# Two softmax attentions in a Trainium2 kernel: the heads taken one at a time, or two at a time in the two halves of the TensorE array

## The chip, the cores and the metric

The kernel runs on one core of one Trainium2 chip. The metric is the device time of one execution in microseconds (us). Times are medians of several runs; the rows shown come from one more execution, taken by the hardware profiler.

## What is computed

The program computes two transformer blocks on 256 tokens of width 1024, in fp32. Only the attention of the second block matters here. Two groups of 8 heads of 64 channels each attend causally over the 256 tokens; the second group adds a decay made of the cumulated logarithms of a forget gate:

```python
    s_own = jnp.einsum('bhcd,bhld->bhcl', qi, k_own).astype(jnp.float32) * scale
    s_own = jnp.where(causal, s_own, -jnp.inf)
    p = jax.nn.softmax(jnp.concatenate([s_sel, s_own], axis=-1), axis=-1)
...
    c = jnp.cumsum(log_f, axis=-1)
...
        s = (jnp.einsum('bhqd,bhkd->bhqk', qi, k).astype(jnp.float32) * scale
             + cq[..., None] - c[:, :, None, :])
        s = jnp.where(kpos[None, :] <= qpos[:, None], s, -jnp.inf)
        p = jax.nn.softmax(s, axis=-1).astype(v.dtype)
        return jnp.einsum('bhqk,bhkd->bhqd', p, v)
```

With 256 tokens there is one block of keys, so the first group is plain causal attention.

## The kernel before, in words

**The dense layers.** `linear` multiplies activations with weights that stream from HBM in units of 128x1024 numbers. ScalarE rounds a unit into a high part (`whi`, L204), VectorE, or GpSimd where `pool_k` says so, subtracts it into a low part (`wlo`, L207, L209), and TensorE forms every product in three passes of 256 columns (L229 to L231, `mm`). A unit is 24 such matmuls. The buffers `raw`, `whi` and `wlo` hold three units each.

**The attention steps.** The attention is a generator. `spawn(generator, rate)` puts it beside the dense layers; after each unit `linear` calls `tick(1/2)`, which adds half of the rate to a counter and runs one step of the generator, up to its next `yield`, for each whole number in it. `drain` runs what is left. So a step's instructions stand between two units of the dense layer, and a scheduler then orders each engine's instructions. The first attention (heads A, tiles `qa`, `ka`, `vta`) runs beside the layer that makes `qb`, `kb` and the values `vtb`; the second (heads B, tiles `qb`, `kb`, `vtb`) beside the layer that makes the gates `gt`. Head h has its 64 channels in rows 0 to 63 of chunk h // 2 if h is even, in rows 64 to 127 if it is odd.

**One step before** works at four heads at once, as a pipeline:

- scores of head h (L1319): 128 queries against 128 keys and 128 queries against 256 keys, with 64 of the array's 128 rows. For B the gate follows into the same PSUM tile (L1321), with 40 rows. The products are of full fp32 numbers, and each stands in the trace as two instructions.
- transposes of head h - 2 (L1326), three of 128x128, copied from PSUM by ScalarE (L1328).
- softmax of head h - 1: VectorE scales and masks out of PSUM (L1333), takes row extremes (L1336), ScalarE exponentiates with sums (L1337), VectorE inverts the sums and scales (L1339, L1341).
- value products of head h - 3 (L1348, L1349): the 64 channels of an even head come out in columns 0 to 63 of the array, of an odd head in columns 64 to 127. After an odd head the pair's sums are split into `oh` and `ol` (L1351, L1352).

```python
            if h < 8:
                c, par = divmod(h, 2)
                R, F = slice(64 * par, 64 * par + 64), slice(64 * par, 64 * par + 40)
```

**The gate's preparation.** `fox_c` (L1285) turns the eight gate rows into cumulated sums on VectorE (L1296, L1297) and ends in two rounds of a VectorE scaling `fw` (L1302), a GpSimd product `selh` over 8x2048 numbers (L1303), and a VectorE scaling `frh` (L1304). On VectorE these stand between the weight units and the first softmaxes of A.

Of the kernel before, what the change touches and what calls it, by code (L numbers as in the profile page):

```python
# [8 lines left out]
FT = mybir.dt.float32  # L9
# [4 lines left out]
AF = mybir.ActivationFunctionType  # L14
OP = mybir.AluOpType
AX = mybir.AxisListType
PSUM = bass.MemoryType.PSUM

P = 128
S = 256  # L20
# [140 lines left out]
class Kernel:  # L161
# [511 lines left out]
    def wkv(self, psum, pw, pA, y):  # L673
# [103 lines left out]
        for n in range(2):  # L777
            yield
            for src, dst in ((bt, mb[n]), (kt, mk[n])):
                for par in range(2):  # L780
                    R = slice(64 * par, 64 * par + 64)
                    ps = psum.tile([P, 2, 2 * P], FT, name="ax")
                    for c in range(2):
                        T.matmul(ps[:, c, :], src[R, c, n * P:(n + 1) * P],
                                 ar[R, c, n].rearrange("p a b -> p (a b)"), start=True, stop=True)
                    V.copy_predicated(dst[:, par], mskb, ps)
# [52 lines left out]
        for n in range(2):  # L839
# [4 lines left out]
            for par in range(2):  # L844
                R = slice(64 * par, 64 * par + 64)
                yp = psum.tile([P, 2, 64], FT, name="ax")
                for c in range(2):
                    T.matmul(yp[:, c, :], mk[n][:, par, c, 0:P], vh(par, c), start=True, stop=n == 0)
                    if n:
                        T.matmul(yp[:, c, :], ar[R, c, n, 0, :], st[R, c, :], start=False, stop=True)  # L850
                SC.activation(ys[:, par], yp, AF.Copy)
# [7 lines left out]
            if n == 0:  # L859
                sp = psum.tile([P, 2, 64], FT, name="ax")  # L860
                for c in range(2):
                    for par in range(2):
                        R = slice(64 * par, 64 * par + 64)
                        T.matmul(sp[R, c, :], bk[:, 0, c, R], us[:, par, c, :], start=True, stop=False)
# [307 lines left out]
    def block2_mix(self):  # L1172
        nc, tc = self.nc, self.tc
        V, SC, G, T = nc.vector, nc.scalar, nc.gpsimd, nc.tensor
        psum = self.psum
        with tc.tile_pool(name="pd", bufs=1) as pd:
# [3 lines left out]
            rot, ct, st, amask = atc[:, 0:128], atc[:, 128:384], atc[:, 384:640], atc[:, 640:1024]  # L1180
# [7 lines left out]
            qa, ka, qb, kb = (t(n, [P, 4, S]) for n in ("qa", "ka", "qb", "kb"))  # L1188
            vt = {n: t("vt" + n, [P, 2, 512]) for n in "ab"}
            gt = t("gt", [P, 16, S])  # L1190
            oh, ol = t("oh", [P, 2, 4, S], FR), t("ol", [P, 2, 4, S], FR)
# [51 lines left out]
            self.selh = selh  # L1243
            self.linear(psum, hh, hl, 12, 8, evac, outer=True)
            self.linear(psum, hh, hl, 1, 8, lambda n, ps: evac(n + 12, ps), groups=[1])
            self.spawn(self.attention(psum, pd, qa, ka, vt["a"], amask, None, oh[:, 0], ol[:, 0]), 1.5)
            self.linear(psum, hh, hl, 12, 8, lambda n, ps: evac(n + 13, ps))
            self.drain()
            self.spawn(self.attention(psum, pd, qb, kb, vt["b"], amask, self.fox, oh[:, 1], ol[:, 1]), 1.2)
            self.linear(psum, hh, hl, 16, 8, lambda n, ps: evac(n + 25, ps))  # L1250
            merged = t("mg", [P, 8, S])
            mh, ml = t("mh", [P, 8, S], FR), t("ml", [P, 8, S], FR)
# [54 lines left out]
    def attention(self, psum, pd, q, k, vt, amask, fox, oh, ol):  # L1307
        nc = self.nc
        V, SC, G, T = nc.vector, nc.scalar, nc.gpsimd, nc.tensor
        parts = ((0, 128), (128, 256))  # L1310
        sp, s, pp, op = {}, {}, {}, {}
        for step in range(8 + 3):
            h = step
            if h < 8:
                c, par = divmod(h, 2)
                R, F = slice(64 * par, 64 * par + 64), slice(64 * par, 64 * par + 40)
                sp[h] = psum.tile([P, 384], FT, name="ax")
                for i, (o, n) in enumerate(parts):
                    T.matmul(sp[h][:, o:o + n], q[R, c, i * P:(i + 1) * P], k[R, c, 0:n], start=True, stop=fox is None)  # L1319
                    if fox:  # L1320
                        T.matmul(sp[h][:, o:o + n], fox[0][F, h, i * P:(i + 1) * P], fox[1][F, 0:n], start=False, stop=True)  # L1321
            h = step - 2
            if 0 <= h < 8:
                pp[h] = psum.tile([P, 384], FT, name="ax")
                for b in range(3):
                    T.transpose(pp[h][:, b * P:(b + 1) * P], s[h][:, b * P:(b + 1) * P], self.ident)  # L1326
                pt = pd.tile([P, 384], FT, name="pt", bufs=3)
                SC.activation(pt, pp[h], AF.Copy)  # L1328
                pp[h] = pt
            h = step - 1  # L1330
            if 0 <= h < 8:
                s[h] = pd.tile([P, 384], FT, name="sc", bufs=3)
                V.scalar_tensor_tensor(s[h], sp[h], -0.125, amask, op0=OP.mult, op1=OP.add)  # L1333
                mx = pd.tile([P, 4], FT, name="mx", bufs=3)
                for i, (o, n) in enumerate(parts):
                    V.tensor_reduce(mx[:, i:i + 1], s[h][:, o:o + n], axis=AX.X, op=OP.min)  # L1336
                    SC.activation(s[h][:, o:o + n], s[h][:, o:o + n], AF.Exp, bias=mx[:, i:i + 1], scale=-1.0,  # L1337
                                  accum_out=mx[:, 2 + i:3 + i])
                V.reciprocal(mx[:, 2:4], mx[:, 2:4])  # L1339
                for i, (o, n) in enumerate(parts):  # L1340
                    V.tensor_scalar(s[h][:, o:o + n], s[h][:, o:o + n], mx[:, 2 + i:3 + i], None, op0=OP.mult)  # L1341
            h = step - 3
            if 0 <= h < 8:
                c, par = divmod(h, 2)
                R = slice(64 * par, 64 * par + 64)
                if par == 0:
                    op[c] = psum.tile([P, S], FT, name="ax")
                T.matmul(op[c][R, :], vt[:, 0, h * 64:(h + 1) * 64], pp[h][:, 0:256], start=True, stop=False)  # L1348
                T.matmul(op[c][R, 128:256], vt[:, 1, h * 64:(h + 1) * 64], pp[h][:, 256:384], start=False, stop=True)  # L1349
                if par:  # L1350
                    SC.activation(oh[:, c, :], op[c], AF.Copy)  # L1351
                    V.tensor_tensor(ol[:, c, :], op[c], oh[:, c, :].bitcast(FT), op=OP.subtract)  # L1352
            yield

    def peer(self):
# [271 lines left out]
```

## Time and profile before

| what | value |
|---|---|
| median of 3 runs | 1610.3 us (1606.66 to 1611.36) |
| the profiled execution | 1612.27 us, of which the span of its instructions 1610.5 us |
| TensorE busy | 1555.3 us, 97% of the span |
| VectorE busy | 1141.2 us, 71% |
| ScalarE busy | 840.0 us, 52% |
| GpSimd busy | 367.3 us, 23% |
| TensorE clock, mean of the execution | 0.985 of full speed |
| first scores of A, last value product of B (starts) | 588.7 and 717.2 us of the span |

Busy time says how much of the span an engine had an instruction in flight. TensorE's instructions overlap, so what one costs is the distance from its start to the next one's start, not its duration.

### The profile page before, as it was taken

The numbers are of one execution on the slowest core, as the hardware profiler recorded it, in microseconds if no ns is written. First come the engines' busy times: TensorE is split into PE (matmuls) and PEld (weight loads), VectorE is DVE, ScalarE is ACT, GpSimd is POOL, SyncE is SP. The second block draws the span as 40 slices with busy tenths as digits, with TensorE's granted clock in tenths as the row PEclk, the third lists the DMA queues.
The fourth block names the chain that finished last, engine by engine and source line by source line (L and its number), as shares of the span: only waits on it lengthen the run. The fifth ranks groups of instructions, "written<-read, shape, count | busy, mean of one in ns | idle before, by whom it ended". The sixth has DMA issues, their size and how long they took to land. (4 is left out here: it accounts for less than half of the span.)

```text
span 1610.5 us, 28420 instructions
## 1 busy us (share of the span) xinstructions
PE 1555.3 (97%) x11206; PEld 1444.6 (90%) x11206; DVE 1141.2 (71%) x1800; ACT 840.0 (52%) x1393; POOL 367.3 (23%) x319
## 2 busy tenths in 40 slices
PE   7998999999999989999999999999999999999997
PEld 5897889999999978989999999999999788888886
DVE  7689876688656676557679887888899555555555
ACT  4562223556644445545354547777776445444443
POOL 7516753416500020003784510000000000000000
PEclk9899899999999999999999999999999999999999
DMA  8555446576665643445655565544445666666663
GB/s 333 181 154 156 132 148 191 176 221 223 176 192 177 204 132 118 131 118 165 214 157 176 180 184 149 153 145 145 148 144 155 190 205 185 193 194 195 193 193 125
DMA packets 75446, 279.87 MB, mean 174 GB/s; under 512 B 8368, under 2 KB 8880, under 8 KB 73648
## 3 DMA queue, kind: packets, MB, share of 16 engines
q1 hardware_dynamic: 75312, 278.05, 56.4%
q8 instruction: 88, 1.44, 0.4%
q14 instruction: 46, 0.38, 0.1%
HBM read 275.92 MB, written 2.10 MB: 173 GB/s over the span
## 5 line engine op out<-in xcount | busy, mean ns | idle before, releaser
L204 ACT ACTIVATE whi<-raw 128x1024 fp32r<-128x1024 f32 x453 | 479.0, 1058 | 582.7 <-PE mm L230 240.2
L207 DVE TENSOR_TENSOR wlo<-raw,whi 128x1024 fp32r<-128x1024 f32 (+2 forms) x413 | 501.5, 1216 | 266.5 <-ACT whi L204 265.3
L229 PE MATMUL mm<-hh,whi 128*128 128x256 f32 x1816 | 525.1, 289 | 1.2 <-ACT uD L464 1.2
L231 PE MATMUL mm<-hh,wlo 128*128 128x256 f32 x1816 | 516.8, 285 | 6.0 <-DVE wlo L207 5.2
L230 PE MATMUL mm<-hl,whi 128*128 128x256 f32 x1816 | 513.3, 283 | 1.1 <-DVE hl L1450 0.7
L231 PEld LDWEIGHTS mm<-hh,wlo 128*128 128x128 f32 x1816 | 346.3, 191 | 8.9 <-DVE wlo L207 6.2
L229 PEld LDWEIGHTS mm<-hh,whi 128*128 128x128 f32 x1816 | 345.3, 190 | 9.2 <-issue 7.4
L230 PEld LDWEIGHTS mm<-hl,whi 128*128 128x128 f32 x1816 | 346.5, 191 | 2.9 <-issue 1.4
L209 POOL TENSOR_TENSOR wlo<-raw,whi 128x256 fp32r<-128x256 f32 (+2 forms) x112 | 185.8, 1664 | 138.9 <-ACT whi L204 85.9
L1484 PE MATMUL ax<-whi,ah 128*128 128x512 f32 x512 | 158.7, 391 | 3.9 <-ACT ah L330 3.9
L1484 PE MATMUL ax<-whi,al 128*128 128x512 f32 x512 | 158.5, 391 | 0.0
L1484 PE MATMUL ax<-wlo,ah 128*128 128x512 f32 x512 | 158.0, 390 | 0.0
L1484 PEld LDWEIGHTS ax<-whi,ah 128*128 128x128 f32 x512 | 96.0, 188 | 23.8 <-ACT ah L330 4.1
L1484 PEld LDWEIGHTS ax<-whi,al 128*128 128x128 f32 x512 | 96.5, 189 | 20.5 <-DVE al L331 0.4
L1484 PEld LDWEIGHTS ax<-wlo,ah 128*128 128x128 f32 x512 | 96.4, 188 | 20.1
L1408 ACT ACTIVATE om<-xres,tg 128x128 f32<-128x128 f32 x256 | 84.9, 392 | 1.0 <-DVE xres L1405 1.0
L231 PE MATMUL ax<-hh,wlo 128*128 128x258 f32 x256 | 72.8, 284 | 1.5 <-DVE wlo L207 1.5
L229 PE MATMUL mm<-fh,whi 128*128 128x256 f32 x256 | 73.0, 285 | 0.0
L231 PE MATMUL mm<-fh,wlo 128*128 128x256 f32 x256 | 72.9, 285 | 0.0
L230 PE MATMUL mm<-fl,whi 128*128 128x256 f32 x256 | 72.9, 285 | 0.0
L229 PE MATMUL ax<-hh,whi 128*128 128x258 f32 x256 | 72.7, 284 | 0.0
L230 PE MATMUL ax<-hl,whi 128*128 128x258 f32 x256 | 72.2, 282 | 0.0
(526 smaller groups left out, 2486.1 us busy)
## 6 DMA issues: line engine op xcount, KB each, us to landing
raw<-in_wts SPq DMA_DIRECT2D x453, 512.0 KB, 3.7
raw<-in_ada SPq DMA_DIRECT2D x24, 512.0 KB, 3.8
araw<-in_ada SPq DMA_DIRECT2D x8, 1024.0 KB, 7.9
w0r<-in_w SPq DMA_DIRECT2D x8, 576.0 KB, 8.9
araw<-in_ada SPq DMA_DIRECT2D x8, 512.0 KB, 4.9
x<-in_x SPq DMA_DIRECT2D x1, 1024.0 KB, 5.3
mb<-in_x SPq DMA_DIRECT2D x2, 512.0 KB, 5.5
selh<-in_att SPq DMA_DIRECT2D x1, 1024.0 KB, 7.2
```

Source lines behind the costliest of these rows:

```text
L204: nc.scalar.activation(hi, raw, AF.Copy)
L207: nc.vector.tensor_tensor(lo[:, :c], raw[:, :c], hi[:, :c].bitcast(FT), op=OP.subtract)
L209: nc.gpsimd.tensor_tensor(lo[:, c:], raw[:, c:], hi[:, c:].bitcast(FT), op=OP.subtract)
L229: mm(ps, wh, xh, start=start, stop=False, **kw)
L230: mm(ps, wh, xl, start=False, stop=False, **kw)
L231: mm(ps, wl, xh, start=False, stop=stop, **kw)
L1408: SC.activation(om[:, j, :], oe[:, j, :], AF.Copy, scale=it["g"][:, t0 + j:t0 + j + 1])
L1484: T.matmul(acc[t][c], a[:, u, z], w[:, c * 512:(c + 1) * 512], start=i + u == 0 and n == 0, stop=i + u == P - 1 and n == 2)
```

## The change

The heads are taken in pairs. One pass of the new loop issues the scores of both heads of a chunk (`scores`), then the transposes of the pair before (`turn`); the next step the two softmaxes (`soft`), and the third the value products of the pair before (`weigh`). Within `scores` and `weigh` the even and the odd head alternate, so that products that use different halves of the array's rows (scores, gate) or columns (values) stand next to each other. The scaled scores get four buffers in place of three. A pass has three yields in place of one per head, and the rates of the two generators are raised from 1.5 to 2.05 and from 1.2 to 1.65. The number and size of the instructions stay the same.

```diff
-            self.spawn(self.attention(psum, pd, qa, ka, vt["a"], amask, None, oh[:, 0], ol[:, 0]), 1.5)
+            self.spawn(self.attention(psum, pd, qa, ka, vt["a"], amask, None, oh[:, 0], ol[:, 0]), 2.05)
...
-            self.spawn(self.attention(psum, pd, qb, kb, vt["b"], amask, self.fox, oh[:, 1], ol[:, 1]), 1.2)
+            self.spawn(self.attention(psum, pd, qb, kb, vt["b"], amask, self.fox, oh[:, 1], ol[:, 1]), 1.65)
...
+        half = [slice(0, 64), slice(64, 128)]
+        sp, s, pt = {}, {}, {}
+
+        def scores(c):
+            for a in range(2):
+                sp[a] = psum.tile([P, 384], FT, name="ax")
+            for i, (o, n) in enumerate(parts):
+                for a, R in enumerate(half):
+                    T.matmul(sp[a][:, o:o + n], q[R, c, i * P:(i + 1) * P], k[R, c, 0:n], start=True, stop=fox is None)
+                if fox:
+                    for a in range(2):
+                        F = slice(64 * a, 64 * a + 40)
+                        T.matmul(sp[a][:, o:o + n], fox[0][F, 2 * c + a, i * P:(i + 1) * P], fox[1][F, 0:n],
+                                 start=False, stop=True)
+
+        def soft(a):
+            s[a] = pd.tile([P, 384], FT, name="sc", bufs=4)
...
+        def turn():
+            for a in range(2):
+                pp = psum.tile([P, 384], FT, name="ax")
                 for b in range(3):
...
+                    T.transpose(pp[:, b * P:(b + 1) * P], s[a][:, b * P:(b + 1) * P], self.ident)
+                pt[a] = pd.tile([P, 384], FT, name="pt", bufs=3)
+                SC.activation(pt[a], pp, AF.Copy)
+
+        def weigh(c):
+            op = psum.tile([P, S], FT, name="ax")
+            for i, (z, o) in enumerate(((slice(0, S), slice(0, S)), (slice(128, S), slice(256, 384)))):
+                for a, R in enumerate(half):
+                    h = 2 * c + a
+                    T.matmul(op[R, z], vt[:, i, h * 64:(h + 1) * 64], pt[a][:, o], start=i == 0, stop=i == 1)
+            SC.activation(oh[:, c, :], op, AF.Copy)
+            V.tensor_tensor(ol[:, c, :], op, oh[:, c, :].bitcast(FT), op=OP.subtract)
+
+        for c in range(4 + 1):
+            if c < 4:
+                scores(c)
+            if c:
+                turn()
+            yield
+            if c < 4:
+                soft(0)
+                soft(1)
+            yield
+            if c:
+                weigh(c - 1)
             yield
```

How instructions move is shown at three places. The first is TensorE in the middle of the second attention. Before, a step of four heads:

```order
L231 MATMUL mm<-hh,wlo 128x256
L1319 MATMUL ax<-kb,qb 128x128
L1321 MATMUL ax<-frh,selh 128x128
L1319 MATMUL ax<-kb,qb 128x256
L1321 MATMUL ax<-frh,selh 128x256
L1326 MATMUL ax<-main,sc 128x128 x3
L1348 MATMUL ax<-pt,vtb 64x256
L1349 MATMUL ax<-pt,vtb 64x128
L229 MATMUL mm<-hh,whi 128x256
```

With the change, the scores and transposes of pairs, and apart from them the value products of a pair:

```order
L231 MATMUL mm<-hh,wlo 128x256
L1319 MATMUL ax<-kb,qb 128x128 x2
L1323 MATMUL ax<-frh,selh 128x128 x2
L1319 MATMUL ax<-kb,qb 128x256 x2
L1323 MATMUL ax<-frh,selh 128x256 x2
L1342 MATMUL ax<-main,sc 128x128 x6
L229 MATMUL mm<-hh,whi 128x256
...
L231 MATMUL mm<-hh,wlo 128x256
L1351 MATMUL ax<-pt,vtb 64x256 x2
L1351 MATMUL ax<-pt,vtb 64x128 x2
L229 MATMUL mm<-hh,whi 128x256
```

An entry "x2" is one product of each head of the pair. Over both attentions, what stood in 21 places between dense matmuls stands in 17.

The second place is TensorE before the change at the end of the first attention, where the value products of its last two heads, 6 and 7, happen to stand one behind the other:

```order
L229 MATMUL mm<-hh,whi 128x256
L1348 MATMUL ax<-pt,vta 64x256
L1349 MATMUL ax<-pt,vta 64x128
L1348 MATMUL ax<-pt,vta 64x256
L1349 MATMUL ax<-pt,vta 64x128
L230 MATMUL mm<-hl,whi 128x256
```

Head 6 comes first with both of its products, then head 7; with the change the two heads alternate.

The third is VectorE where the first softmaxes of A meet the gate's preparation. Before:

```order
L1296 TENSOR_TENSOR fz<-fz,fu 8x256
L1237 TENSOR_TENSOR qb<-mm,r_6040 128x512
L1297 SCALAR_TENSOR_TENSOR fu<-main,fz 8x256
L207 TENSOR_TENSOR wlo<-raw,whi 128x1024
L1302 TENSOR_SCALAR fw<-fu 8x256
L1304 TENSOR_SCALAR frh<-fu 8x256
L1302 TENSOR_SCALAR fw<-fu 8x256
L1304 TENSOR_SCALAR frh<-fu 8x256
L1333 SCALAR_TENSOR_TENSOR sc<-ax,atc 128x384
L1336 TENSOR_REDUCE mx<-sc 128x1 x2
L1333 SCALAR_TENSOR_TENSOR sc<-ax,atc 128x384
L207 TENSOR_TENSOR wlo<-raw,whi 128x1024
```

With the change, from the first reduction of head 0 to the unit behind the softmax of head 1's start:

```order
L1331 TENSOR_REDUCE mx<-sc 128x1
L1302 TENSOR_SCALAR fw<-fu 8x256
L1304 TENSOR_SCALAR frh<-fu 8x256
L1302 TENSOR_SCALAR fw<-fu 8x256
L1304 TENSOR_SCALAR frh<-fu 8x256
L1237 TENSOR_TENSOR qb<-mm,r_6040 128x512
L1334 RECIPROCAL mx<-mx 128x2
L1328 SCALAR_TENSOR_TENSOR sc<-ax,atc 128x384
L1336 TENSOR_SCALAR sc<-sc,mx 128x128
L1336 TENSOR_SCALAR sc<-sc,mx 128x256
L1331 TENSOR_REDUCE mx<-sc 128x1 x2
L207 TENSOR_TENSOR wlo<-raw,whi 128x1024
```

The scaling of head 0 out of PSUM and its two reductions now stand ahead of the first `fw`; the `qb` write and a weight unit that stood ahead of `fw` stand elsewhere. The unit's subtraction now stands between head 0's softmax and the end of head 1's.

## Rows read from the trace of the kernel before

**Rows 1.** The page's first part, TensorE: busy, share of the span, instructions.

```profile
PE 1555.3 (97%) x11206; PEld 1444.6 (90%) x11206; DVE 1141.2 (71%) x1800; ACT 840.0 (52%) x1393; POOL 367.3 (23%) x319
```

**Rows 2.** Busy time by stretch, 612 to 718 us: engines, clock, DMA share, GB/s.

```profile
612.00:718.00 106.00, 106.00 (x770) 92.24 (x769) 62.36 (x121) 54.35 (x113) 0.00 (x0) 1.00 0.40 120
```

**Rows 3.** Timeline of TensorE, one step of A: start us, us, engine, line, operation.

```profile
622.01 0.92 PE L1319 MATMUL ax<-ka,qa 64*128 64x128 f32 x4
622.86 0.55 PE L1326 MATMUL ax<-main,sc 128*128 128x128 f32 x3
623.34 0.65 PE L1348 MATMUL ax<-pt,vta 128*64 128x256 f32 x2
...
624.13 0.38 PE L229 MATMUL mm<-hh,whi 128*128 128x256 f32 x1
624.35 0.28 PE L230 MATMUL mm<-hl,whi 128*128 128x256 f32 x1
624.47 0.28 PE L231 MATMUL mm<-hh,wlo 128*128 128x256 f32 x1
```

**Rows 4.** Timeline of TensorE, one step of B, to the start of its transposes.

```profile
686.27 0.28 PE L231 MATMUL mm<-hh,wlo 128*128 128x256 f32 x1
686.48 0.48 PE L1319 MATMUL ax<-kb,qb 64*128 64x128 f32 x2
...
687.98 0.55 PE L1326 MATMUL ax<-main,sc 128*128 128x128 f32 x3
```

**Rows 5.** Timeline of TensorE, the value products of heads 6 and 7 of A.

```profile
643.58 0.66 PE L1348 MATMUL ax<-pt,vta 128*64 128x256 f32 x4
...
644.39 0.39 PE L230 MATMUL mm<-hl,whi 128*128 128x256 f32 x1
```

**Rows 6.** Timeline of TensorE, another stage: products in both halves of the rows.

```profile
119.25 1.14 PE L784 MATMUL ax<-ar,bt 64*128 64x256 f32 x8
120.22 1.13 PE L784 MATMUL ax<-ar,kt 64*128 64x256 f32 x8
```

**Rows 7.** Timeline of TensorE around the first transposes of A.

```profile
596.51 0.92 PE L1319 MATMUL ax<-ka,qa 64*128 64x128 f32 x4
603.22 0.95 PE L1326 MATMUL ax<-main,sc 128*128 128x128 f32 x3 [5.80 <-DVE sc L1341]
603.83 0.56 PE L229 MATMUL mm<-hh,whi 128*128 128x256 f32 x1
...
611.70 0.48 PE L1319 MATMUL ax<-ka,qa 64*128 64x128 f32 x2
```

**Rows 8.** Busy time by stretch, as rows 2, 605 to 610 us.

```profile
605.00:610.00 5.00, 5.00 (x32) 5.00 (x31) 2.72 (x10) 2.47 (x6) 0.00 (x0) 0.67 0.43 152
```

**Rows 9.** Timeline of VectorE, 589 to 603 us.

```profile
589.46 0.67 DVE L1237 TENSOR_TENSOR qb<-mm,r 128x512 f32<-128x512 f32 x1
...
590.66 1.19 DVE L207 TENSOR_TENSOR wlo<-raw,whi 128x1024 fp32r<-128x1024 f32 x1
...
592.38 4.58 DVE L1302 TENSOR_SCALAR fw<-fu 8x256 f32<-8x256 f32 x1
...
597.90 0.61 DVE L1336 TENSOR_REDUCE mx<-sc 128x1 f32<-128x128 f32 x2
...
598.89 3.82 DVE L207 TENSOR_TENSOR wlo<-raw,whi 128x1024 fp32r<-128x1024 f32 x1
...
602.90 0.54 DVE L1341 TENSOR_SCALAR sc<-sc,mx 128x128 f32<-128x128 f32 x2
```

**Rows 10.** Timeline of GpSimd, 592 to 602 us.

```profile
592.13 4.68 POOL L1303 TENSOR_TENSOR selh<-selh,fw 8x2048 f32<-8x2048 f32 x1 [19.91 <-DVE fw L1302]
597.11 4.53 POOL L1303 TENSOR_TENSOR selh<-selh,fw 8x2048 f32<-8x2048 f32 x1 [0.29 <-DVE fw L1302]
```

**Rows 11.** Timeline of VectorE, one softmax of B.

```profile
651.80 0.55 DVE L1333 SCALAR_TENSOR_TENSOR sc<-ax,atc 128x384 f32<-128x384 f32 x1
...
653.93 0.55 DVE L1341 TENSOR_SCALAR sc<-sc,mx 128x128 f32<-128x128 f32 x2
```

More of the change, by code (lines that the diff above doesn't have):

```diff
@@ L1310, in attention @@
         parts = ((0, 128), (128, 256))
[L1311 to L1324, printed above, removed]
-                for b in range(3):
[L1326 to L1352, printed above, removed]
@@ new lines, in soft @@
+        def soft(a):
+            s[a] = pd.tile([P, 384], FT, name="sc", bufs=4)
+            V.scalar_tensor_tensor(s[a], sp[a], -0.125, amask, op0=OP.mult, op1=OP.add)
+            mx = pd.tile([P, 4], FT, name="mx", bufs=3)
+            for i, (o, n) in enumerate(parts):
+                V.tensor_reduce(mx[:, i:i + 1], s[a][:, o:o + n], axis=AX.X, op=OP.min)
+                SC.activation(s[a][:, o:o + n], s[a][:, o:o + n], AF.Exp, bias=mx[:, i:i + 1], scale=-1.0,
+                              accum_out=mx[:, 2 + i:3 + i])
+            V.reciprocal(mx[:, 2:4], mx[:, 2:4])
+            for i, (o, n) in enumerate(parts):
+                V.tensor_scalar(s[a][:, o:o + n], s[a][:, o:o + n], mx[:, 2 + i:3 + i], None, op0=OP.mult)
```

## The prediction

> **What bounds the kernel now.** I read the page's busy times first: TensorE is busy for 97% of the span [rows 1]. Then busy time by stretch over the attentions: from 612 to 718 us TensorE has no idle time at full clock, while VectorE is busy for 62.36 of the 106 us, ScalarE for 54.35, and the DMA engines for 0.40 [rows 2]. So from 612 us on every microsecond that TensorE saves there is a microsecond of the end, and since the rest of the kernel hangs on TensorE as well [rows 1], nothing later takes it back. The exception is the start. There TensorE stands idle for 5.80 us before the first transposes and then runs slowly [rows 7, 8]; what it saves ahead of that wait only lengthens the wait.
>
> The timeline of TensorE gives prices, as distances between starts. Dense matmuls come every 0.12 us; scores take 0.85 us per head of A, transposes 0.48, value products 0.79, and the first dense matmul behind them 0.22, thus 0.10 more than usual [rows 3]. The step into the scores takes 0.21 in place of 0.12, so 0.09 more; scores and gate of B take 1.50 [rows 4]. A step of A so costs 0.09 + 0.85 + 0.48 + 0.79 + 0.10 = 2.31 us, one of B 2.96 us. The gate's products add 1.50 - 0.85 = 0.65 us for 768 streamed columns (twice 128 and twice 256): 0.85 ns a column, 0.11 us for a transpose that needs no new entry.
>
> **Do the halves overlap?** The trace has both cases. The value products of heads 6 and 7 of A stand together already: eight instructions in 644.39 - 643.58 = 0.81 us [rows 5], where the four of one head take 0.79 [rows 3]. The second head is free. For row halves there is line 784: eight instructions of 256 columns, in both halves, take 120.22 - 119.25 = 0.97 us [rows 6]; at 0.85 ns a column one behind the other they would take 1.74. So I price a pair of scores as one head's (0.85, with gate 1.50) and a pair of value products at 0.81. The Trainium skill (TensorE: Matmul & The Clock Gate, "What overlaps and what doesn't") says that matmuls start and end strictly in program order. By that rule the value products of heads 6 and 7 could not overlap as they do, since all of head 6's come first in the program; by rows 5 the trace does not agree, and the sum goes by the rows. What the rule would give is the first rival.
>
> **The sum.** Entering costs 0.09 and leaving 0.10. Two heads' transposes take 0.48 + 3 x 0.11 = 0.81.
>
> - A before: two places with scores alone (1.04 each), one with scores and transposes (1.52), five full steps (11.55), one with transposes, values, transposes (1.94), and one with the value products of heads 6 and 7 (1.00): 18.1 us.
> - A after: one place with scores alone (1.04), three with a pair's scores and the transposes of the pair before (0.09 + 0.85 + 0.81 + 0.10 = 1.85 each), three with values alone (1.00 each), one with values and transposes (1.81): 11.4 us. Value transposes of the dense layer (L1229) that shared a place before now stand alone: 0.2. Gain 6.5 us.
> - B before: two places with scores and gate (1.69 each), one with transposes (2.17), five full steps (14.8), two with transposes and values (1.46 each), one with values (0.98): 24.2 us.
> - B after: scores and gate once (1.69), three times with transposes (2.50 each), transposes alone (1.00), values alone four times (1.00 each): 14.2 us. Gain 10.0 us.
>
> Together 16.5 us; about 4 of them are places and changes of kind saved, the rest overlap.
>
> **The wait at the start.** Its cause is VectorE. While GpSimd multiplies `selh` for 4.68 and 4.53 us [rows 10], one `fw` takes 4.58 us and one weight subtraction 3.82 in place of 1.19; only then is the first softmax scaled, and the transposes start right behind it at 603.22 [rows 7, 9]. Products of GpSimd thus hold VectorE operations whose operands all lie in SBUF; a reduction inside the second one took its usual time (0.61) [rows 9]. The change takes `qb` (0.67) and a weight unit (1.19) from ahead of the first `fw` and puts two reductions (0.61) there, so the second product ends 1.25 us earlier, at about 600.4. Behind it come the scaling of head 0 (0.54, if held like `fw`), two reductions (0.61), a weight unit (1.19), an inversion and the scaling of head 1 (0.54): head 1's transposes start near 603.4, head 0's have gone into the wait, and the dense matmuls resume at about 604.0 in place of 603.83. Loss 0.2 us. If the scaling is not held, they resume 1 us earlier. Up to there the same number of dense matmuls is done, and TensorE's attention work is 3.6 us before (two scores alone, one with transposes) and 2.9 after; these 0.7 us are swallowed by the wait.
>
> The 48 dense matmuls behind the wait take 611.70 - 603.83 = 7.87 us [rows 7] for the usual 5.7, at a mean granted clock of 0.67 [rows 8], thus mostly at the lower level, 1.2 GHz in place of 2.4. The idle time ahead is similar after (about 4.5 us, the transposes of head 0, and 2 us more), so I keep this cost. Its bounds: 2.2 us gained if the clock stays up, 1 us lost if it stays down longer.
>
> Behind the transposes queue the dense matmuls, so a late softmax would stall everything. After the start I cost this at nothing: a softmax takes 653.93 + 0.55 - 651.80 = 2.7 us [rows 11], two behind each other 5.4 at most and with a weight unit 6.6; between the scores of a pair and its transposes lie at least 48 dense matmuls, a value pair and four transposes, about 7.4 us, mostly 9.5. No DMA is moved past another, and VectorE and ScalarE get the same instructions.
>
> Sum: 16.5 - 0.7 - 0.2 = **15.6 us**. The profiled execution took 1612.27 us and so becomes 1596.7. It lies above all three runs shown; from their median of 1610.3 the same gain gives **1594.7 us**.
>
> **The rivals.**
>
> - *Program order binds.* If TensorE starts products strictly in order, only the second instruction of one head overlaps the first of the next, and each pair of scores or values loses the time of one 256-column instruction, 0.22 us: 16 pairs, 3.5 us, so 1598.2. Rows 5 speak against it, at full length. Chance 8%.
> - *Two softmaxes come too late.* One softmax behind the other on VectorE makes each pair's transposes wait. It decides from a chain longer than 7.4 to 9.5 us. At 1 us for each of the seven pairs behind the start the time is 1601.7. For it speaks that VectorE's order puts weight units, which wait for ScalarE, between the two; against it, 44 idle us of VectorE in 106 [rows 2]. Chance 7%.
> - *The halves do not overlap.* Then 12.3 us of the 16.5 stay away (4 pairs of scores at 0.65, 4 with gate at 1.30, 7 of values at 0.65; heads 6 and 7 of A overlapped before), and 1607.0 remains. Rows 5 and 6 show the opposite for both kinds. Chance 3%.
> - *Swapping halves costs an entry*, the slower side. If every change between the even and the odd head is paid like a change of kind (0.09 + 0.10), and nothing overlaps, the alternating order has 3 changes in each pair of scores, 3 in each of values, 7 in each with gate: 64 changes, 12.2 us, against the 3.3 us that remain: 1619.2. It decides from 0.05 us a change. The eight value products of rows 5 have no room for such a price, but their program order does not alternate. Chance 3%.
>
> **How the numbers follow.** The forecast has 79%. Its own bounds are 1 us and 2.2 us better at the start, 1 us worse, and the scatter of the runs, 3.6 us below and 1.1 above their median. From 1589.5 (the better bounds and part of the scatter) to 1602 the range holds the forecast and the first two rivals in nearly all their size and leaves out the last two. A difference of 0.3% is 4.8 us, about what a measurement of this kernel can tell from no change. Faster by more: forecast, first rival and most of the second, 93%. Within: the third rival and a second that costs more than 11 us, 4%. Slower: the fourth, 3%.
>
> **What would show it.** In the profile after, the scores of a pair should stand as one group of 8 instructions with 0.85 us to the transposes, with gate 1.50; a pair of values 0.81. TensorE should stay without idle time from the second pair on, and the last value product should lie some 15 us earlier. The first transposes should still wait for VectorE, in two parts around those of head 0. Wrong would be: starts of the two heads a full instruction apart (first or third rival), gaps ahead of later transposes that end with VectorE's scaling (second), or groups longer than two heads' separate ones (fourth).

## The result, and the profile after

The changed kernel takes 1591.0 us (median of 4 runs, 1589.85 to 1593.79), the kernel before, run beside it, 1608.5 us (4 runs, 1603.28 to 1611.36): a ratio of 0.9894, with a 95% interval of 0.9877 to 0.9911, or 17.4 us. The forecast was 1594.7 us. The profiled execution of the changed kernel is the slowest of the four (1593.79 us, span 1592.0), so its stages are compared below, not its end.

TensorE's busy time falls by 16.3 us with the same number of instructions [rows 1]; that of VectorE, ScalarE and GpSimd moves by 4.2 us at most:

```profile
PE 1539.0 (97%) x11206; PEld 1436.0 (90%) x11206; DVE 1145.4 (72%) x1800; ACT 838.3 (53%) x1393; POOL 365.1 (23%) x319
```

The attention stage runs from the first transpose of L1229 to the first product with `mh`. On TensorE's timeline these rows mark it, first in the kernel before, then in the changed one (the first row of each is the start of a group of four instructions, of which the view holds two and one):

```profile
576.39 0.38 PE L1229 MATMUL ax<-main,qraw 128*128 128x128 f32 x2
...
736.56 0.36 PE L229 MATMUL mm<-mh,whi 128*128 128x256 f32 x1 [0.22 <-DVE mt L1259]
```

```profile
575.32 0.27 PE L1229 MATMUL ax<-main,qraw 128*128 128x128 f32 x1
...
718.63 0.36 PE L229 MATMUL mm<-mh,whi 128*128 128x256 f32 x1 [0.22 <-DVE mt L1259]
```

The stage takes 160.17 us before and 143.31 after: 16.9 us saved. Outside it the program is the same; ahead of it the two executions differ by 1.07 us (576.39 and 575.32).

Now TensorE's timeline of the changed kernel: a pair of A with the transposes of the pair before, a pair of values, and a pair of B, to be held against [rows 3 to 5].

```profile
614.06 0.28 PE L231 MATMUL mm<-hh,wlo 128*128 128x256 f32 x1
614.26 0.93 PE L1319 MATMUL ax<-ka,qa 64*128 64x128 f32 x8
615.12 0.88 PE L1342 MATMUL ax<-main,sc 128*128 128x128 f32 x6
615.75 0.36 PE L229 MATMUL mm<-hh,whi 128*128 128x256 f32 x1
615.96 0.28 PE L230 MATMUL mm<-hl,whi 128*128 128x256 f32 x1
...
621.62 0.87 PE L1351 MATMUL ax<-pt,vta 128*64 128x256 f32 x8
622.42 0.39 PE L229 MATMUL mm<-hh,whi 128*128 128x256 f32 x1
...
652.44 0.49 PE L1319 MATMUL ax<-kb,qb 64*128 64x128 f32 x4
...
653.95 0.87 PE L1342 MATMUL ax<-main,sc 128*128 128x128 f32 x6
```

Eight score instructions take 0.86 us to the transposes, where the four of one head took 0.85 [rows 3]. Eight value instructions take 0.80 (0.79 for four), a pair with gate 653.95 - 652.44 = 1.51 (1.50 for one head [rows 4]). The second head is free in all three kinds. Six transposes take 0.63, against 0.48 for three in front of value products [rows 3].

After the start TensorE has no idle time until B is done; the window that answers to [rows 2]:

```profile
612.00:702.00 90.00, 90.00 (x767) 83.88 (x766) 58.87 (x115) 50.86 (x107) 0.00 (x0) 1.00 0.49 142
```

The start itself, that is TensorE around the first transposes, answers to [rows 7]:

```profile
594.40 0.93 PE L1319 MATMUL ax<-ka,qa 64*128 64x128 f32 x8
599.49 0.70 PE L1342 MATMUL ax<-main,sc 128*128 128x128 f32 x3 [4.17 <-DVE sc L1336]
601.89 0.88 PE L1342 MATMUL ax<-main,sc 128*128 128x128 f32 x3 [1.71 <-DVE sc L1336]
602.42 0.56 PE L229 MATMUL mm<-hh,whi 128*128 128x256 f32 x1
...
610.43 0.87 PE L1351 MATMUL ax<-pt,vta 128*64 128x256 f32 x8
```

The wait is 4.17 + 1.71 = 5.88 us in two parts, where it was 5.80 in one, and the 48 dense matmuls behind it take 8.01 us (7.87 before). Busy time by stretch shows them at a low clock, as [rows 8] did:

```profile
600.00:605.00 5.00, 3.29 (x17) 3.12 (x16) 4.96 (x9) 3.55 (x8) 0.00 (x0) 0.54 0.45 119
605.00:610.00 5.00, 5.00 (x36) 5.00 (x36) 4.43 (x13) 2.94 (x9) 0.00 (x0) 0.77 0.63 196
```

VectorE tells why, with GpSimd's two products beside it; these answer to [rows 9, 10]:

```profile
590.09 4.59 DVE L1302 TENSOR_SCALAR fw<-fu 8x256 f32<-8x256 f32 x1
...
595.02 0.69 DVE L1237 TENSOR_TENSOR qb<-mm,r 128x512 f32<-128x512 f32 x1
595.63 0.15 DVE L1334 RECIPROCAL mx<-mx 128x2 f32<-128x2 f32 x1
...
596.16 3.54 DVE L1336 TENSOR_SCALAR sc<-sc,mx 128x128 f32<-128x128 f32 x2
```

```profile
589.84 4.68 POOL L1303 TENSOR_TENSOR selh<-selh,fw 8x2048 f32<-8x2048 f32 x1 [18.68 <-DVE fw L1302]
594.82 4.53 POOL L1303 TENSOR_TENSOR selh<-selh,fw 8x2048 f32<-8x2048 f32 x1 [0.30 <-DVE fw L1302]
```

The second `fw` (alone 0.27) and the first head's scaling (alone 0.54) end 0.16 and 0.35 us behind the end of a product of GpSimd. `qb`, which reads PSUM, runs inside the second product at its usual 0.69. Not every operation on SBUF alone is held: the inversion at 595.63 runs inside the second product in its usual 0.15 us, as a reduction did in the kernel before [rows 9].

### The profile page after: what moved, and what is told of

It reads as the page before. It is cut to its first block, busy times and chain, and to the rows that moved or that the text cites. A ratio compares the mean times of both kernels' runs of the same rounds, so it can differ in the third digit from the quotient of the medians.

```text
span 1592.0 us, 28434 instructions
## 1 busy us (share of the span) xinstructions
PE 1539.0 (97%) x11206; PEld 1436.0 (90%) x11206; DVE 1145.4 (72%) x1800; ACT 838.3 (53%) x1393; POOL 365.1 (23%) x319
## 3 DMA queue, kind: packets, MB, share of 16 engines
q8 instruction: 88, 1.44, 0.4%
```

## The experiments

Eight kernels, each timed against the kernel before, which ran beside each of three groups of runs at 1608.5, 1609.0 and 1609.8 us, so the ratios compare kernels better than medians do. The stage is measured as above, in the profiled execution. It leaves out what varies ahead of it and behind it. One part of it varies too: the 48 dense matmuls behind the wait, 8.01 us in the changed kernel, took 8.30 with the same rows, 7.47 with the same columns, 7.33 head after head, 8.20 with the gate behind its score and 7.80 with transposes between.

| kernel | median, us | ratio to before, 95% interval | stage, us | against |
|---|---|---|---|---|
| before | 1608.5 | 1 | 160.17 | |
| changed | 1591.0 | 0.9894 (0.9877 to 0.9911) | 143.31 | before: -16.9 |
| same rows | 1600.0 | 0.9942 (0.9928 to 0.9956) | 150.15 | changed: +6.8 |
| same columns | 1598.3 | 0.9938 (0.9925 to 0.9952) | 147.86 | changed: +4.6 |
| head after head | 1593.7 | 0.9908 (0.9894 to 0.9921) | 144.98 | changed: +1.7 |
| no product | 1583.2 | 0.9841 (0.9826 to 0.9856) | 134.56 | changed: -8.8 |
| before, no product | 1601.8 | 0.9952 (0.9937 to 0.9967) | 151.95 | before: -8.2 |
| gate behind score | 1595.0 | 0.9910 (0.9895 to 0.9926) | 143.93 | changed: +0.6 |
| transposes between | 1598.5 | 0.9935 (0.9920 to 0.9949) | 150.94 | changed: +7.6 |
| product on VectorE | 1587.9 | 0.9869 (0.9851 to 0.9887) | 137.51 | changed: -5.8 |

### Is it the halves? The same rows, the same columns

```diff
-T.matmul(sp[a][:, o:o + n], q[R, c, i * P:(i + 1) * P], k[R, c, 0:n], ...)
+T.matmul(sp[a][:, o:o + n], q[half[0], c, i * P:(i + 1) * P], k[half[0], c, 0:n], ...)
...
-                        F = slice(64 * a, 64 * a + 40)
+                        F = slice(0, 40)
```

> The changed kernel, but both heads of a pair take their score and gate products from rows 0 to 63; the order, the places and the number of instructions stay. (Head 1's scores are so computed from head 0's rows; the values are as in the changed kernel.) Theory (the halves overlap, and this makes most of the gain): the second head has to run behind the first, so a pair of scores takes 0.85 + 0.65 = 1.50 us, a pair with gate 1.50 + 1.30 = 2.80. The first two pairs of A lie ahead of the first transposes and are swallowed by the wait there; 2 x 0.65 + 4 x 1.30 = 6.5 us are left: about 1597.5 us, a ratio to the kernel before of 0.993. Rival (the pairs gain by standing together, whichever rows they use, because places and changes of kind are saved): no difference to the changed kernel, 1591 us, ratio 0.989.

The same pairs on TensorE's timeline, one of A and one of B, with both heads in the same rows:

```profile
612.98 1.57 PE L1319 MATMUL ax<-ka,qa 64*128 64x128 f32 x8
614.48 0.87 PE L1342 MATMUL ax<-main,sc 128*128 128x128 f32 x6
...
653.74 0.71 PE L1319 MATMUL ax<-kb,qb 64*128 64x128 f32 x4
...
656.56 0.88 PE L1342 MATMUL ax<-main,sc 128*128 128x128 f32 x6
```

A pair takes 1.50 us in place of 0.86, with gate 2.82 in place of 1.51: 0.65 and 1.30 more, as priced. The stage is 6.8 us longer for an expected 6.5. The medians differ by 9 us and the ratios by 7.7, somewhat more than expected and well away from the rival's 0.

```diff
-            op = psum.tile([P, S], FT, name="ax")
+            op = psum.tile([64, 2, S], FT, name="ax")
...
-                    T.matmul(op[R, z], vt[:, i, h * 64:(h + 1) * 64], pt[a][:, o], start=i == 0, stop=i == 1)
-            SC.activation(oh[:, c, :], op, AF.Copy)
-            V.tensor_tensor(ol[:, c, :], op, oh[:, c, :].bitcast(FT), op=OP.subtract)
+                    T.matmul(op[:, a, z], vt[:, i, h * 64:(h + 1) * 64], pt[a][:, o], start=i == 0, stop=i == 1)
+            for a, R in enumerate(half):
+                SC.activation(oh[R, c, :], op[:, a, :], AF.Copy)
+                V.tensor_tensor(ol[R, c, :], op[:, a, :], oh[R, c, :].bitcast(FT), op=OP.subtract)
```

> The changed kernel, but both heads of a pair write their value products to columns 0 to 63 of the array, head 0 first; they are copied out head by head (two small copies and two subtractions in place of one of each). Theory: a pair of values takes 0.81 + 0.65 = 1.46 us, 8 pairs give 5.2 us more: about 1596.2 us, ratio 0.992. Rival (only standing together counts): 1591 us, ratio 0.989. A third possibility is that the additional copies delay something: then the trace shows TensorE waiting for ScalarE or VectorE after 612 us.

A pair of values with both heads in the same columns, on TensorE's timeline:

```profile
607.47 1.51 PE L1351 MATMUL ax<-pt,vta 128*64 128x256 f32 x8
608.91 0.39 PE L229 MATMUL mm<-hh,whi 128*128 128x256 f32 x1
```

1.44 us in place of 0.80: 0.64 a pair, 8 pairs 5.1. The stage is 4.6 us longer; the missing 0.5 us are the dense matmuls behind the wait, 7.47 us in this execution. By the ratios the time is 7.1 us longer, more than the stage shows, and the 2.5 us between are not explained. After the start TensorE waits no more than before, so the additional copies cost nothing there. The overlap of the halves is thus shown for rows and for columns, at the prices of the prediction.

### Does the order within a pair matter?

```diff
-            for i, (o, n) in enumerate(parts):
-                for a, R in enumerate(half):
+            for a, R in enumerate(half):
+                for i, (o, n) in enumerate(parts):
...
-            for i, (z, o) in enumerate(((slice(0, S), slice(0, S)), (slice(128, S), slice(256, 384)))):
-                for a, R in enumerate(half):
-                    h = 2 * c + a
+            for a, R in enumerate(half):
+                h = 2 * c + a
+                for i, (z, o) in enumerate(((slice(0, S), slice(0, S)), (slice(128, S), slice(256, 384)))):
```

> The changed kernel, but within a pair all products of the even head come first and then all of the odd one, as for heads 6 and 7 of A in the kernel before; nothing else differs. Theory (products start as soon as their own half is free, also ahead of earlier ones in the program): a pair takes the same 0.85, 1.50 and 0.81 us and the time stays at 1591 us, ratio 0.989. Rival (products start in program order, and the alternating order is what makes them overlap): each pair of scores or of values loses at least one instruction of 256 columns, 0.22 us, a pair with gate about 0.22 to 0.65: 3.5 to 5.2 us, 1594.5 to 1596, and starts of the two heads lie a full instruction apart.

Half right. Pairs without gate and pairs of values keep their price (0.86 and 0.81 us). A pair with gate, where the gate products now follow the scores of their own head, does not, on TensorE's timeline:

```profile
639.53 0.49 PE L1319 MATMUL ax<-kb,qb 64*128 64x128 f32 x2
639.85 0.38 PE L1322 MATMUL ax<-frh,selh 40*128 40x128 f32 x2
640.08 0.59 PE L1319 MATMUL ax<-kb,qb 64*128 64x256 f32 x4
640.41 0.48 PE L1322 MATMUL ax<-frh,selh 40*128 40x128 f32 x3
640.63 0.38 PE L1319 MATMUL ax<-kb,qb 64*128 64x256 f32 x1
640.73 0.37 PE L1322 MATMUL ax<-frh,selh 40*128 40x256 f32 x1
...
641.59 0.39 PE L229 MATMUL mm<-hh,whi 128*128 128x256 f32 x1
```

The pair takes 641.59 - 639.53 = 2.06 us; with all eight instructions of a head on their own it would be 2.8, in the changed kernel it is 1.5. The even head's first four instructions stand alone; from 640.08 on the two heads mix. The group of four at 640.08 holds two of the even head's second scores and two of the odd head's first, which the program has behind two more gate instructions of the even head. So instructions for the other half do start ahead of their turn, but only past a few.

When the odd head's first instruction starts, at 640.08, three earlier ones of the even head have not started. From 639.97 on there were four, and it did not start, although its half was idle and the profile shows no wait that ends there. The program's order alone can't give this mix, since the two instructions of one product are neighbours in it: those of the even head's second gate product start at 640.51, inside the group of three, and at 640.73, and instructions of the odd head start between them.

Four pairs at 0.55 are 2.2 us, which is what the time shows (1593.7, where theory said 1591 and the rival 1594.5 or more). The stage is 1.7 us longer only, because the dense matmuls behind the wait took 0.7 us less in this execution. The Trainium skill (TensorE: Matmul & The Clock Gate, "What overlaps and what doesn't") has matmuls start strictly in program order; the group at 640.08 does not agree.

Two readings of the 0.55 us were left: the reach of TensorE, or score and gate into one place that follow each other at once.

```diff
-                if fox:
-                    for a in range(2):
+                    if fox:
```

> The changed kernel with the gate products in another order: for each stretch of columns score and gate of the even head, then score and gate of the odd one. (With all products of the even head first, score and gate twice each, a pair with gate took 2.05 us in place of 1.50, while pairs without gate and values lost nothing.) Theory: a product can start ahead of its turn, but only past about four matmul records (two instructions); past the eight records of an even head with gate it could not reach. Here never more than four stand in between: 1.50 us a pair and the time of the changed kernel, 1591 us, ratio 0.989. Rival (it is the order of score and gate, two products into one place that follow each other at once, that costs): the same 2.05 us a pair, 2.2 us in all, ratio 0.9905, and in the trace starts of the two heads that do not alternate.

The pair on TensorE's timeline:

```profile
641.99 0.50 PE L1319 MATMUL ax<-kb,qb 64*128 64x128 f32 x4
642.31 0.40 PE L1322 MATMUL ax<-frh,selh 40*128 40x128 f32 x4
...
643.60 0.39 PE L229 MATMUL mm<-hh,whi 128*128 128x256 f32 x1
```

643.60 - 641.99 = 1.61 us: 0.10 above the changed kernel, not 0.55. Each group belongs to both heads, although the program has four instructions of one head between those of the other. The reach explains both runs; what the 0.10 us are stays open. By the median, 1595.0 us, the rival would look right, since the interval begins above 0.989. The trace speaks against it: the pair costs 0.10 us and not 0.55, and the stage is 0.6 us longer, 0.4 of it the four pairs. The median lies 4.0 us above that of the changed kernel; the kernel before was 1.3 us slower beside these runs too, and what puts the rest there stays open.

### Must the two heads be neighbours?

```diff
...
-            if c < 4:
-                scores(c)
-            if c:
-                turn()
+            for a in range(2):
+                if c < 4:
+                    scores(c, a)
+                if c:
+                    turn(a)
```

> The changed kernel with the transposes of the pair before put one head each behind the scores of each head (scores, three transposes, scores, three transposes), so that something on the whole array stands between the two halves; the places among the dense matmuls and the number of instructions stay, also the values. Theory (only neighbours overlap): each pair with transposes falls back to two heads apart, as before: 2 x 1.32 in place of 1.66 us for two pairs of A, 2 x 1.98 in place of 2.32 for three of B, and about 0.9 us for the second pair of A, whose second scores now come behind the wait: 2.0 + 4.9 + 0.9 = 7.8 us, 1599 us, ratio 0.994. The first pair of B has no transposes between and stays at 1.50. Rival (TensorE reaches past three transposes to the free half): no loss or under 2 us, ratio 0.989 to 0.9905.

`scores` and `turn` now each take one head, and with it a head's scores and gate products stand together. The pair of A, on TensorE's timeline:

```profile
615.03 0.92 PE L1318 MATMUL ax<-ka,qa 64*128 64x128 f32 x4
615.88 0.55 PE L1340 MATMUL ax<-main,sc 128*128 128x128 f32 x3
616.36 0.92 PE L1318 MATMUL ax<-ka,qa 64*128 64x128 f32 x4
```

Each head costs its 0.85 again. The five pairs with transposes between cost 6.9 us more, as expected. The stage is 7.6 us longer for an expected 7.8, but that the sums agree so well is luck: the first pair of B, which has no transposes between, was expected at 1.50 us and takes 2.06, since its heads follow each other as in the kernel head after head, and the start costs 0.1 us and not 0.9. Three transposes are no more than the three instructions that a head was seen to reach past, but they use the whole array, the odd head's half too. So nothing like them may stand between the two heads.

### The wait at the start

The row's own forget sum is the same for a whole row of scores and drops out of the softmax, so the two products can be left out.

```diff
...
-            c = w[b:b + 8]
-            V.tensor_scalar(c, u, 8.0, None, op0=OP.mult)
-            nc.gpsimd.tensor_tensor(lh[b:b + 8], lh[b:b + 8], c[:, None, :].to_broadcast([8, 8, S]), op=OP.mult)
```

> The changed kernel without GpSimd's two products into selh and the two fw scalings that feed them. What it leaves out is the row's own forget sum, a number that is the same for a whole row of scores and so drops out of the softmax. Theory (VectorE was held by the products, the transposes waited for it, and the idle time made the clock fall): the first scaling of VectorE takes 0.55 us instead of 3.54, the first pair's transposes start right behind the second pair's scores; 4.17 + 1.71 us of idle time and about 2.3 us of slow matmuls go: 8 us, about 1583 us, ratio 0.984. Rival 1 (VectorE's queue is late at this place by itself): a wait of 2 to 4 us stays, 1587 us, ratio 0.987. Rival 2 (the clock falls there without idle time too): only 5.9 us, 1585 us, and a granted clock well under 1 from 600 to 610 us.

VectorE's first scaling, TensorE's first transposes and busy time by stretch without the products:

```profile
587.70 0.54 DVE L1333 TENSOR_SCALAR sc<-sc,mx 128x128 f32<-128x128 f32 x2
```

```profile
590.56 0.93 PE L1316 MATMUL ax<-ka,qa 64*128 64x128 f32 x8
591.42 0.88 PE L1339 MATMUL ax<-main,sc 128*128 128x128 f32 x6
592.05 0.36 PE L229 MATMUL mm<-hh,whi 128*128 128x256 f32 x1
```

```profile
590.00:600.00 10.00, 10.00 (x87) 9.09 (x85) 9.35 (x20) 6.35 (x15) 0.00 (x0) 1.00 0.58 168
600.00:605.00 5.00, 5.00 (x45) 4.54 (x44) 2.90 (x7) 2.31 (x5) 0.00 (x0) 1.00 0.60 193
```

The scaling takes 0.54 in place of 3.54, the transposes follow the scores at once, the granted clock stays at 1.00, from 605 to 610 us too. The time is 1583.2 us, 7.8 below the changed kernel. The rivals expected 1587 and 1585; the second lies inside the interval of the time, and it is the granted clock that excludes it. This is the fastest kernel of the study: 0.9841 of the kernel before.

> The kernel before without the same two products of GpSimd and their fw scalings (left out is again the row's own forget sum, which drops out of the softmax). With the changed kernel and the changed kernel without products this makes four kernels. Theory: the wait at the start and the overlap of the halves have nothing to do with each other. The kernel before loses its idle time of 5.80 us and some 2.2 us of slow matmuls, 8.0 to 8.5 us, about 1600.5 us, ratio 0.995, and the change is then worth 17.4 us between the two kernels without products. Rival (a part of the gain of the change came from the wait at the start, which two heads at a time passed better): the change is worth clearly more or less than that between the kernels without products, by over 2 us.

Its edit is the same three lines. The wait is gone here too: the scores ahead of the first transposes start at 597.27, and the transposes 0.85 us behind them, on TensorE's timeline:

```profile
598.12 0.55 PE L1323 MATMUL ax<-main,sc 128*128 128x128 f32 x3
```

The stage is 8.2 us shorter. Between the two kernels without products the change is worth 151.95 - 134.56 = 17.4 us of stage, 18.6 between the medians and 17.9 by the ratios. Wait and overlap are independent but for about half a microsecond.

To tell being held from having too much to do, VectorE got the products as well:

```diff
-            nc.gpsimd.tensor_tensor(lh[b:b + 8], lh[b:b + 8], c[:, None, :].to_broadcast([8, 8, S]), op=OP.mult)
+            V.tensor_tensor(lh[b:b + 8], lh[b:b + 8], c[:, None, :].to_broadcast([8, 8, S]), op=OP.mult)
```

> The changed kernel with the two products computed by VectorE instead of GpSimd, at the same places in the program. Theory (a product of GpSimd holds VectorE's operations with all operands in SBUF): VectorE now has two products more, each about 8 x 0.27 = 2.2 to 2.4 us by the 256 elements of fw, but the 4.59 us of the second fw and the 3.54 us of the first scaling fall to 0.27 and 0.54. Together 2.5 us less: the first transposes start some 2.5 us earlier against the first pair's scores and 1588.5 us result, ratio 0.988. Rival (VectorE has too much to do there, and the long fw and scaling only show that): 4.5 us more work for VectorE make the wait longer by about as much, 1595 us, ratio 0.992.

VectorE, TensorE, and busy time by stretch of this kernel:

```profile
587.93 2.28 DVE L1303 TENSOR_TENSOR selh<-selh,fw 8x2048 f32<-8x2048 f32 x1
590.22 0.28 DVE L1302 TENSOR_SCALAR fw<-fu 8x256 f32<-8x256 f32 x1
...
594.31 0.54 DVE L1336 TENSOR_SCALAR sc<-sc,mx 128x128 f32<-128x128 f32 x2
```

```profile
592.24 0.93 PE L1319 MATMUL ax<-ka,qa 64*128 64x128 f32 x8
594.64 0.70 PE L1342 MATMUL ax<-main,sc 128*128 128x128 f32 x3 [1.47 <-DVE sc L1336]
```

```profile
594.00:612.00 18.00, 16.39 (x135) 15.15 (x136) 16.76 (x41) 10.39 (x29) 0.00 (x0) 1.00 0.59 175
```

With 4.6 us more work VectorE is done earlier: the first transposes start 2.40 us behind the scores in place of 5.09. So it was held, and not overloaded. The Trainium skill (SBUF — State Buffer, "SBUF: two separate sides") says that VectorE and GpSimd share a pair of ports, which an instruction that needs it holds to its end while one of the other engine that needs it blocks; the 4.59 and 3.54 us above and their disappearance agree. The stage gains 5.8 us, more than the 2.5 expected. TensorE is idle for 1.47 and 0.98 us (the latter for a weight subtraction) in place of 5.88, 3.4 less; here its order changed as well, with 14 dense matmuls between the transposes of the two heads. The rest is the clock, which stays up. The medians differ by 3.1 us only (4.0 by the ratios), near the expectation. In which of the other executions the clock falls after the wait can't be seen.

## Why the prediction was right

The forecast lies 3.7 us above the result. Half of this is the kernel before, whose median of 1610.3 us became 1608.5 with a fourth run, and half the gain, 17.4 us for 15.6. The terms, by the same rows as the stage; measured is, for each group of attention instructions, the distance from the last dense matmul ahead to the second one behind it, less two distances of dense matmuls (for 614.26: 615.96 - 614.06 - 2 x 0.12 = 1.66). The places that hold the wait are taken at their price in the kernels without products, 1.32 and 1.66.

| term, us | predicted | measured |
|---|---|---|
| A before, A after | 18.1, 11.6 | 17.6, 10.8 |
| B before, B after | 24.2, 14.2 | 23.9, 13.3 |
| gain of both | 16.5 | 17.4 |
| lost at the start | 0.9 | 0.5 |
| stage | 15.6 | 16.9 |

The 0.5 us lost at the start are 0.7 swallowed by the wait, less 0.3 by which the dense matmuls resume earlier, and 0.1 of the clock.

- **What bounds the kernel**: right. TensorE has no idle time from 612 us on, and what the stage saves, the end saves.
- **The halves overlap**: right at every price: 0.86, 1.51 and 0.80 us a pair; without overlap 0.65, 1.30 and 0.64 more. That is the 12.3 us of the text.
- **Places and changes of kind**: 17.4 - 12.3 = 5.1 us where the text had 4. This is a remainder; no run takes it apart. The mis-sized term is the transposes, 0.81 us a pair by 0.48 + 3 x 0.11; they take 0.63. The 0.48 of [rows 3] runs to the start of the value products and so holds the change to those, which in the new order is paid with the values. Six transposes cost 0.105 each and no entry. This also put the kernel before 0.8 us too high. The 0.2 us for the value transposes of L1229 standing alone did not come: they cost 0.44 us shared or alone.
- **The wait at the start**: its cause, its two parts, the end of the second product (599.35 + 1.07 = 600.42, forecast 600.4) and the swallowed 0.7 us were right. The dense matmuls resume at 602.42, which with the 1.07 us by which the stage begins earlier is 603.49 on the clock of before, where 604.0 was forecast. Head 0's scaling is two instructions; the first was held inside the second product and ended 0.08 us behind it, and the next reduction started 0.27 us behind the product, where 0.54 was counted. The rest of the 0.5 us lies in the steps after it, which the forecast added by their durations, though a step starts before the one ahead of it has ended (601.27 is ahead of 600.14 + 1.21 by 0.08). That operations on SBUF alone are held was too wide, as the inversion shows; no term hung on it.
- **The clock**: kept, right. 8.01 us for the 48 matmuls, 7.87 before. That they agree to 0.14 us is luck in part: in the experiments with the wait they took 7.33 to 8.30.
- **Later waits cost nothing**: right. One small thing was missed: the last values of A stand seven dense matmuls behind their transposes and take 0.24 us more than other pairs (1.23 for 0.99). Their odd head starts at 635.91, right behind ScalarE's copy of its transposes, which ends at 635.86.
- **The rivals**: that halves do not overlap, that swapping costs an entry and that softmaxes come late are excluded by the pairs' prices and the idle time. Program order binds in part: the alternating order is not needed for scores and values, but with gate the same products head by head cost 0.55 us a pair.

## What to carry to other kernels

Where two products of this size use different halves of the array's rows or columns, the second one was free here when nothing that needs the whole array stood between. Alternate them, since TensorE was seen to reach past three instructions only. Price an instruction by the distance between starts in the order that the new program has: a distance taken ahead of a change of kind holds that change. And before buying time on the engine that bounds, look at why it idles: here two products of a helper engine, 9.2 us together and not themselves on the path, held another engine and cost 8 us, nearly half of what the change gave.

## What had not been expected of the hardware

- An instruction for the other half of the rows starts ahead of three earlier ones that have not started, and did not with four: head by head, a pair without gate (four instructions a head) overlaps wholly, one with gate (eight a head) takes 2.06 us in place of 1.51. That the limit is a number of instructions was not tried apart.
- An idle time of 4.17 us and another of 1.71 went along with a granted clock of 0.54 of full speed from 600 to 605 us, thus mostly the lower level, 1.2 GHz; after idle times of 1.47 and 0.98 it stayed at 1.00.
- Inside GpSimd's second product a scaling on VectorE took 3.54 us for 0.54, and an inversion just ahead of it, whose operands lie in SBUF as well, its usual 0.15. VectorE forms the same product of 8x2048 numbers in 2.28 us, as was expected, for which GpSimd takes 4.68.
